# Deferring the gating of the first two channel tiles of a ConvFFN by one tile, and pinning four low halves to other places

## The chip, the cores and the metric

The kernel runs on one core of a Trainium2 chip. The metric is the device time of one execution in microseconds; before, three runs gave a median of 1300.59 us (1300.02 to 1301.46). The engines are called here as in the profile: PE (TensorE's matrix multiplications), PEld (its weight loads), DVE (VectorE), ACT (ScalarE), POOL (GpSimd) and SP (SyncE, which issues most DMAs).

## The reference, cut to what matters

One decoder layer in float32 on 16 meta tokens and 1024 tokens, model width 1024. The part that the change touches is the end of the mixing block and the ConvFFN:

```
mix = concat([y_diff, y_hgrn]) @ w_out                # out projection, 1024 x 1024
h   = h + rmsnorm(mix, ln_mix_post)
a   = rmsnorm(h, ln_ffn_pre)
u   = a @ w_ffn_up                                    # 1024 -> 2 * 2816
u   = causal depthwise conv over tokens, width 3, + conv_b
gate, up = split(u)
y   = (gelu_tanh(gate) * up) @ w_ffn_down             # 2816 -> 1024
h   = h + rmsnorm(y, ln_ffn_post)
```

`y_diff` is a differential attention with four heads, `y_hgrn` a gated linear recurrence (HGRN2) with four heads; both are computed ahead of this part.

## The kernel before

**Products in three passes.** Each float32 operand of a multiplication is split into a high half in the PE's reduced format (a cast on ACT, `uh`, `woh`, `t` high) and a low half, raw minus high (a subtraction on DVE or POOL, `ul`, `wol`, `t` low; the function `split`). A product is three matmuls, high times high, high times low and low times high (lines 1398, 1399 and 1400 in the up projection, 1028, 1030 and 1032 in the out projection). The low halves are wanted a matmul or two after the high ones.

**The out projection.** `load_wo(n)` loads column half n of `w_out` in eight tiles `wor{n}_{k}` and splits them into `woh{n}_{k}` and `wol{n}_{k}`. PE's products `py` and `pz` of half 0 run in gaps of the recurrence (whose gate products `hq`, `kr` are made by DVE and read by the small matmuls `pl`, `pd`); half 1 follows near 565 us of the profile. The recurrent heads' decay factors `tt`, `t2` are on POOL.

**The up projection.** The 2816 channels are 22 tiles of 128, each with a gate and an up side, and the tokens are two halves, p = 0 (2 x 258 columns) and p = 1 (2 x 256). Tile 0 is done plainly: `plain_unit` makes `pq` in four products for each token half, and ACT copies them to `ug0_p` and `uu0_p`. Tiles 1 to 21 use a fast 2 x 2 block scheme with seven products instead of eight (`unit`): `prep(7*ft + j)` makes the weight operand of product j of tile ft (`uh`, `ul`; the sums `ws1` to `ws4` of raw quarter tiles `ra{ft}_{11,12,21,22}` are POOL's), and `t_sums` and `t_split` make the eight token operands `t{p}_{j}` once, from the transposed activations `at2_p`. The products use three PSUM banks for each token half, in this order of j: `pa`, `pb`, `pc`, `pb`, `pa`, `pb`, `pc`. From the fourth on they accumulate on what lies in the bank, so between two products in one bank an engine has to have read it:

- j = 0 `pa`: ACT copies it to `xu`
- j = 1 `pb`: DVE adds it to `xu` (the trace's `xu<-pb,xu`), before j = 3 may write `pb`
- j = 3 `pb`: DVE makes `u3` (the trace's `u<-pb,xu`) and, with `pc` of j = 2, half of `uu`; j = 5 waits for `u3`
- j = 4 `pa`, j = 5 `pb`, j = 6 `pc`: the other halves of `ug` and `uu`

**Gating.** `gated(ft, p, ug, uu)` takes the finished outputs of a tile and a token half through the convolution: `conv` for each side, an ACT activation (bias and one tap) and two DVE steps (SCALAR_TENSOR_TENSOR, one tap each) in `c0` and `c1`, then the gelu on ACT, the product `c0*c1` on POOL and the store to `gsc` by SP. That is four DVE steps for each call, eight for each tile. `c1` has two buffers, `c0` three.

**What sets the order.** PE's order is written out by the order of the code (`unit` yields after each product, and the loop over `ft` and `j` interleaves two token halves). The order on DVE, ACT, POOL and SP is a scheduler's, over the same code; `tc.issue_after(ins)` holds what is issued inside behind the instruction given. All element-wise work goes through one helper and bears line 58. In before, the loop calls `gated` of a tile at its end, after j = 6, for all tiles; for tile 0 `plain_unit` calls it, token half 0 ahead of the loop and half 1 at j = 1 of tile 1. The weights of tile 2 (`prep(14)` on) are made in places of their own during tile 1:

```
if (ft, j) == (1, 1):
    with tc.issue_after(marks[1, 1].ins):
        next(p1)
    with tc.issue_after(marks["mult"].ins):
        prep(14)
elif ft == 1 and 2 < j < 6:
    with tc.issue_after(marks["last"].ins):
        prep(12 + j)
```

**The down projection** reads the gates back from `gsc` (`g_in`, tiles `gi` with tag `gk` in the pool `dn`), splits them and multiplies with `w_ffn_down` (`pd`).

## Time and profile before

| | |
|---|---|
| time, median of 3 runs (lowest to highest) | 1300.59 us (1300.02 to 1301.46) |
| profiled execution: its own time, its span | 1298.48 us, 1296.7 us |
| mean granted PE clock | 0.993 |
| PE busy | 1261.1 us, 97% |
| DVE busy | 885.1 us, 68% |
| ACT busy | 693.2 us, 53% |
| POOL busy | 485.4 us, 37% |

In the profile a row of a timeline gives the start, the duration, the engine, the line, the operation and its tiles (output<-inputs, buffer numbers left out), a count where neighbours are taken together, and in square brackets the idle time ahead of it and what ended it. The view of waits groups such idle time by the waiting line and the releasing engine: microseconds in total, times, longest. The view by windows gives for each stretch its length, then the busy time of PE, PEld, DVE, ACT and POOL with the number of instructions, the granted PE clock, the DMA share and GB/s. A difference between starts is the better measure of what one operation costs in a train, since durations of neighbours overlap a little. Of the profiled execution the up projection takes roughly from 627 to 1050 us.

### The profile page before, as it was taken

How to read it: one execution, taken by the hardware profiler on the slowest of the kernel's cores; microseconds unless marked ns; L12 is line 12 of the kernel's file. 1: busy time of each engine (PE TensorE's matmuls, PEld its weight loads, DVE VectorE, ACT ScalarE, POOL GpSimd, SP SyncE). 2: the span in 40 equal slices, each digit the busy share in tenths (PEclk: the TensorE clock that was granted, in tenths of full speed). 3: DMA queues.
4: the chain of work that ended last, by engine and by line, in shares of the span. 5: the costliest groups of instructions: out<-in, count | busy, mean ns of one | idle time of the engine just before them, and what ended most of it. 6: DMA issues, size and time to landing. Idle time of an engine off the chain costs nothing.

```text
span 1296.7 us, 26036 instructions
## 1 busy us (share of the span) xinstructions
PE 1261.1 (97%) x10154; PEld 1174.8 (91%) x10154; DVE 885.1 (68%) x1488; ACT 693.2 (53%) x1639; POOL 485.4 (37%) x387
## 2 busy tenths in 40 slices
PE   8999999999999999999997999999999999999996
PEld 7999999999999998768897999999999998878885
DVE  7574646464746564547887778778778786797686
ACT  8465466546654754356754445444445454454553
POOL 5231423242323310352076665765766730010121
PEclk9999999999999999999998999999999999999998
DMA  7335555273634532787322222222222147955363
GB/s 256 95 66 123 88 144 93 74 144 99 122 91 79 123 86 98 247 271 249 112 66 74 82 74 91 82 74 87 85 75 90 66 139 240 343 173 170 90 211 122
DMA packets 116417, 165.04 MB, mean 127 GB/s; under 512 B 10099, under 2 KB 57523, under 8 KB 116294
## 3 DMA queue, kind: packets, MB, share of 16 engines
q1 hardware_dynamic: 93062, 151.84, 36.2%
q0 software_dynamic: 23232, 11.54, 7.5%
q8 instruction: 80, 1.31, 0.4%
q14 instruction: 43, 0.35, 0.1%
HBM read 134.24 MB, written 52.17 MB: 144 GB/s over the span
## 4 chain that ended last, share of the span: by engine, by line
PE 44%; DVE 6%; ACT 2%; issue 1%; DMA 1%; POOL 0%; DVEq 0%; SPq 0%; ACTq 0%; POOLq 0%
PE pd L1567 5%; PE pd L1568 5%; PE pd L1566 5%; PE pb L1398 4%; PE pb L1399 4%; PE pb L1400 4%; PE pa L1399 3%; PE pc L1399 3%; PE pa L1398 3%; PE pc L1398 3%; PE pa L1400 3%; PE pc L1400 3%; DVE c L58 1%; DVE t L58 1%; DVE xh L58 1%
## 5 line engine op out<-in xcount | busy, mean ns | idle before, releaser
L1398 PE MATMUL pb<-t,uh 128*128 128x258 f32 x504 | 142.0, 282 | 8.2 <-DVE xu L58 8.2
L1399 PE MATMUL pb<-t,uh 128*128 128x258 f32 x504 | 142.2, 282 | 0.0
L1400 PE MATMUL pb<-t,ul 128*128 128x258 f32 x504 | 141.4, 281 | 0.0
L1567 PE MATMUL pd<-wl,gh 128*128 128x512 f32 x308 | 120.5, 391 | 1.1 <-DVE wl L58 1.1
L1566 PE MATMUL pd<-wh,gh 128*128 128x512 f32 x308 | 120.0, 390 | 0.0
L1568 PE MATMUL pd<-wh,gl 128*128 128x512 f32 x308 | 120.0, 390 | 0.0
L58 POOL TENSOR_TENSOR c<-c,c 128x514 f32<-128x514 f32 (+1 forms) x44 | 64.2, 1459 | 122.2 <-ACT c L58 118.1
L58 DVE SCALAR_TENSOR_TENSOR c<-uu,cwt,c 128x514 f32<-128x514 f32 (+1 forms) x88 | 95.6, 1087 | 20.5 <-ACT c L58 19.8
L1398 PEld LDWEIGHTS pb<-t,uh 128*128 128x128 f32 x504 | 96.1, 191 | 8.6 <-DVE xu L58 8.6
L1399 PEld LDWEIGHTS pb<-t,uh 128*128 128x128 f32 x504 | 96.1, 191 | 0.0
L1400 PEld LDWEIGHTS pb<-t,ul 128*128 128x128 f32 x504 | 96.1, 191 | 0.0
L1399 PE MATMUL pa<-t,uh 128*128 128x258 f32 (+1 forms) x336 | 94.2, 280 | 0.0
L1399 PE MATMUL pc<-t,uh 128*128 128x258 f32 (+1 forms) x336 | 94.1, 280 | 0.0
L1398 PE MATMUL pa<-t,uh 128*128 128x258 f32 (+1 forms) x336 | 93.9, 279 | 0.0
L1398 PE MATMUL pc<-t,uh 128*128 128x258 f32 (+1 forms) x336 | 93.7, 279 | 0.0
L1400 PE MATMUL pa<-t,ul 128*128 128x258 f32 (+1 forms) x336 | 93.7, 279 | 0.0
L1400 PE MATMUL pc<-t,ul 128*128 128x258 f32 (+1 forms) x336 | 93.6, 278 | 0.0
L58 DVE SCALAR_TENSOR_TENSOR c<-ug,cwt,c 128x514 f32<-128x514 f32 (+1 forms) x88 | 86.2, 980 | 1.2 <-ACT c L58 0.6
L58 ACT CAST uh<-ra 128x512 fp32r<-128x512 f32 x67 | 41.1, 616 | 64.6 <-PE pb L1399 40.2
L58 DVE TENSOR_TENSOR ul<-ra,uh 128x512 fp32r<-128x512 f32 x42 | 40.6, 967 | 47.0 <-ACT uh L58 44.5
L58 POOL TENSOR_TENSOR ul<-ws,uh 128x512 fp32r<-128x512 f32 x42 | 60.2, 1435 | 30.8 <-ACT uh L58 30.8
L1567 PEld LDWEIGHTS pd<-wl,gh 128*128 128x128 f32 x308 | 57.8, 188 | 14.7 <-DVE wl L58 2.8
(389 smaller groups left out, 4171.1 us busy)
## 6 DMA issues: line engine op xcount, KB each, us to landing
ra<-in_wup_dram SPq DMA_DIRECT2D x88, 256.0 KB, 2.8
mp<-msc SPq DMA_DIRECT2D x23, 512.0 KB, 5.8
tsc<-in_wdown_dram SPq DMA_DIRECT2D x44, 256.0 KB, 4.7
wi<-tsc SPq DMA_DIRECT2D x44, 256.0 KB, 3.2
gi<-gsc SPq DMA_DIRECT2D x33, 256.0 KB, 4.6
wi<-in_wdown_dram SPq DMA_DIRECT2D x33, 256.0 KB, 4.8
gsc<-c SPq DMA_DIRECT2D x22, 257.0 KB, 2.1
tsc<-in_wdown_dram POOLq DMA_DIRECT2D x22, 256.0 KB, 6.7
```

The costliest lines, as they stand in the source:

```text
L58: ins = call(*args, **kw)
L1398: T.matmul(pt, hi[:, s], th[:, k], start=(first and k == 0), stop=False, skip_group_check=True)
L1399: T.matmul(pt, hi[:, s], tl[:, k], start=False, stop=False, skip_group_check=True)
L1400: T.matmul(pt, lo[:, s], th[:, k], start=False, stop=(k == 3), skip_group_check=True)
L1566: T.matmul(py, gh[:, s], wh, start=(k == 0 and pr not in (3, 7)), stop=False, skip_group_check=True)
L1567: T.matmul(py, gh[:, s], wl, start=False, stop=False, skip_group_check=True)
L1568: T.matmul(py, gl[:, s], wh, start=False, stop=(k == NH - 1), skip_group_check=True)
```

## The change

The change leaves every computation as it is, and PE's order too. It moves work on the other four engines:

- **Gating of tiles 0 and 1.** The calls of `gated` for tile 0 and tile 1 are put on a list (`later`) and taken from it in the next tile: tile 0's in tile 1 and tile 1's in tile 2, token half 0 after j = 1 and half 1 after j = 3, each held behind the DVE operation that evacuates the product (`marks["last"]`). Tile 2 on gate themselves at their end, as before. So in tile 2 both tile 1's gating and its own are issued.
- **Where tile 1's outputs lie.** `ug1_p` and `uu1_p` are taken from the `gk` tiles of the pool `dn` (four buffers, made 516 wide for it), which otherwise hold gates loaded for the down projection.
- **Weights of tile 2** are prepared by the ordinary calls in the loop; the special places are gone.
- **Low halves pinned.** `wol0_4` to `wol0_7` move from DVE to POOL; the low half of product 4 of tile 1 (`ul11`) moves from POOL to DVE; `prep(7)` to `prep(10)` are held behind the low halves `wol1_4` and `wol1_5`; among the token operands, the lows of quarters `t1_7` and `t1_6` are held ahead of the sums of token half 0 (`t0_2`, `t0_3`, `t0_5`).

On DVE, around product 3 of tile 1 (`xu_1_p` read the bank of product 1, `u3_1_0` that of product 3; `c0_0_0` and `c1_0_0` are the plain tile's convolution steps). Before:

```order
L58 TENSOR_TENSOR ul14_8083<-ra2_11_8072,uh14_8082 128x512
L58 SCALAR_TENSOR_TENSOR c0_0_0_7972<-ug0_0_7645,cwt_84,c0_0_0_7972 128x514
L58 SCALAR_TENSOR_TENSOR c1_0_0_7977<-uu0_0_7646,cwt_84,c1_0_0_7977 128x514
L58 SCALAR_TENSOR_TENSOR c0_0_0_7972<-ug0_0_7645,cwt_84,c0_0_0_7972 128x514
L58 SCALAR_TENSOR_TENSOR c1_0_0_7977<-uu0_0_7646,cwt_84,c1_0_0_7977 128x514
L58 TENSOR_TENSOR xu_1_0_7999<-pb1_0_8033,xu_1_0_7999 128x258
L58 TENSOR_TENSOR xu_1_1_8017<-pb1_1_8047,xu_1_1_8017 128x256
L58 SCALAR_TENSOR_TENSOR c0_0_1_8061<-ug0_1_7825,cwt_84,c0_0_1_8061 128x510
```

and in the changed kernel, from the same low half on:

```order
L58 TENSOR_TENSOR ul14_7997<-ra2_11_7986,uh14_7996 128x512
L58 TENSOR_TENSOR xu_1_0_8003<-pb1_0_8037,xu_1_0_8003 128x258
L58 TENSOR_TENSOR xu_1_1_8021<-pb1_1_8051,xu_1_1_8021 128x256
L58 SCALAR_TENSOR_TENSOR c0_0_0_8065<-ug0_0_7645,cwt_84,c0_0_0_8065 128x514
L58 SCALAR_TENSOR_TENSOR c1_0_0_8070<-uu0_0_7646,cwt_84,c1_0_0_8070 128x514
L58 SCALAR_TENSOR_TENSOR c0_0_0_8065<-ug0_0_7645,cwt_84,c0_0_0_8065 128x514
L58 SCALAR_TENSOR_TENSOR c1_0_0_8070<-uu0_0_7646,cwt_84,c1_0_0_8070 128x514
L58 TENSOR_TENSOR ul15_8079<-ws2_8076,uh15_8078 128x512
L58 TENSOR_TENSOR ul17_8115<-ws3_8112,uh17_8114 128x512
L58 TENSOR_TENSOR u3_1_0_8004<-pb1_0_8037,xu_1_0_8003 128x258
```

The two evacuations have moved ahead of the four steps, and two low halves of tile 2 now stand between the steps and `u3_1_0`; the plain tile's other four steps come behind `u3` and `uu`.

On DVE, around product 3 of tile 2 (`xu_2_0`), with the steps of tile 1 (`c0_1_p`, `c1_1_p`). Before:

```order
L58 TENSOR_TENSOR ug1_1_8015<-pc1_1_8099,xu_1_1_8017 128x256
L58 SCALAR_TENSOR_TENSOR c0_1_0_8235<-ug1_0_7997,cwt_84,c0_1_0_8235 128x514
L58 SCALAR_TENSOR_TENSOR c1_1_1_8264<-uu1_1_8016,cwt_84,c1_1_1_8264 128x510
L58 SCALAR_TENSOR_TENSOR c0_1_1_8259<-ug1_1_8015,cwt_84,c0_1_1_8259 128x510
L58 TENSOR_TENSOR ul21_8281<-ra3_11_8270,uh21_8280 128x512
L58 SCALAR_TENSOR_TENSOR c0_1_1_8259<-ug1_1_8015,cwt_84,c0_1_1_8259 128x510
L58 TENSOR_TENSOR xu_2_0_8286<-pb2_0_8320,xu_2_0_8286 128x258
L58 TENSOR_TENSOR ul22_8351<-ws2_8348,uh22_8350 128x512
```

and in the changed kernel:

```order
L58 TENSOR_TENSOR ul22_8341<-ws2_8338,uh22_8340 128x512
L58 TENSOR_TENSOR xu_2_1_8283<-pb2_1_8313,xu_2_1_8283 128x256
L58 SCALAR_TENSOR_TENSOR c0_1_0_8327<-ug1_0_8000,cwt_84,c0_1_0_8327 128x514
L58 SCALAR_TENSOR_TENSOR c1_1_0_8332<-uu1_0_8001,cwt_84,c1_1_0_8332 128x514
L58 SCALAR_TENSOR_TENSOR c0_1_0_8327<-ug1_0_8000,cwt_84,c0_1_0_8327 128x514
L58 SCALAR_TENSOR_TENSOR c1_1_0_8332<-uu1_0_8001,cwt_84,c1_1_0_8332 128x514
L58 TENSOR_TENSOR ul24_8377<-ws3_8374,uh24_8376 128x512
L58 TENSOR_TENSOR u3_2_0_8266<-pb2_0_8299,xu_2_0_8265 128x258
```

All eight steps of tile 1 stood ahead of `xu_2_0`, the last of them are shown; now `xu_2_0` comes ahead of `ul22`, four steps stand between `xu_2_1` and `u3_2_0`, and the other four behind the evacuations of product 3.

On POOL, at the turn from the out projection to the weights of tile 1 (`wol1_4` is a low half of `w_out`, the rest are sums and a low half of tile 1's weights). Before:

```order
L58 TENSOR_TENSOR wol1_6_7044<-wor1_6_7041,woh1_6_7043 128x512
L58 TENSOR_TENSOR ws1_7819<-ra1_21_7815,ra1_22_7813 128x512
L58 TENSOR_TENSOR ws2_7853<-ws1_7819,ra1_11_7811 128x512
L58 TENSOR_TENSOR ul9_7886<-ws1_7819,uh9_7885 128x512
L58 TENSOR_TENSOR wol1_4_7032<-wor1_4_7029,woh1_4_7031 128x512
L58 TENSOR_TENSOR ws3_7915<-ra1_11_7811,ra1_21_7815 128x512
```

and in the changed kernel:

```order
L58 TENSOR_TENSOR wol1_6_7044<-wor1_6_7041,woh1_6_7043 128x512
L58 TENSOR_TENSOR wol1_4_7032<-wor1_4_7029,woh1_4_7031 128x512
L58 TENSOR_TENSOR ws1_7819<-ra1_21_7815,ra1_22_7813 128x512
L58 TENSOR_TENSOR ws2_7853<-ws1_7819,ra1_11_7811 128x512
L58 TENSOR_TENSOR ws3_7915<-ra1_11_7811,ra1_21_7815 128x512
L58 TENSOR_TENSOR ul9_7886<-ws1_7819,uh9_7885 128x512
```

`wol1_4` has moved ahead of two sums and a low half; on ACT its cast stands ahead of that of `uh9` likewise.

The diff:

```diff
--- before.py
+++ after.py
@@ -156,6 +156,7 @@
             low = (eng or G).tensor_tensor(lo, raw, hi.bitcast(F32), op=ALU.subtract)
         if eng in (None, G):
             lows.append(low)
+        return low
 
     def load_split(src, name, where=None, bufs=4):
         raw = wp.tile([P, 512], F32, tag="wr", name=f"wr_{name}", bufs=WR)
@@ -996,6 +997,8 @@
     ssy = yp.tile([P, NBLK, 4], F32, tag="ssy", name="ssy")
     gpo0 = yp.tile([P, 512], F32, tag="gpo0", name="gpo0")
 
+    wo_low = {}
+
     def load_wo(n):
         res = []
         for k in range(KD):
@@ -1010,10 +1013,10 @@
                 hi = wop.tile([P, 512], F32R, tag="woh", name=f"woh{n}_{k}")
                 lo = wop.tile([P, 512], F32R, tag="wol", name=f"wol{n}_{k}")
             if n == 0:
-                split(hi, lo, raw, V if k else G)
+                split(hi, lo, raw, V if 0 < k < 4 else G)
             else:
                 with tc.issue_after(ends["a"].ins), tc.issue_after(ends["v"].ins):
-                    split(hi, lo, raw, V if k % 2 else G, halved[0])
+                    wo_low[k] = split(hi, lo, raw, V if k % 2 else G, halved[0])
             res.append((hi, lo))
         return res
 
@@ -1167,7 +1170,7 @@
         where = swp if q % 2 else wp
         hi = where.tile([P, 512], F32R, tag="wh", name=f"uh{q}", bufs=4)
         lo = where.tile([P, 512], F32R, tag="wl", name=f"ul{q}", bufs=4)
-        split(hi, lo, src, G if j % 2 == 0 and j else V, marks.get((ft - 1, 0)) if j == 1 else None)
+        split(hi, lo, src, G if j % 2 == 0 and j and (ft > 1 or j != 4) else V, marks.get((ft - 1, 0)) if j == 1 else None)
         made[q] = (hi, lo)
 
     plain = {}
@@ -1262,8 +1265,8 @@
 
     def t_split(p, j, src, where, *tag):
         hi, lo = t_tiles(p, j, where, tag)
-        A.copy(hi, src)
-        V.tensor_tensor(lo, src, hi.bitcast(F32), op=ALU.subtract)
+        marks["cast"] = A.copy(hi, src)
+        marks["low"] = V.tensor_tensor(lo, src, hi.bitcast(F32), op=ALU.subtract)
         tt[p][j] = (hi, lo)
 
     def quarter(p, j):
@@ -1273,15 +1276,21 @@
 
     def t_sums(p, where, last):
         b11, b12, b21, b22 = (quarter(p, j) for j in (0, 7, 4, 6))
-        V.tensor_tensor(b11, b12, b11, op=ALU.subtract)
+        cast, low = marks["quarters"]
+        with tc.issue_after(low.ins) if p else nullcontext():
+            V.tensor_tensor(b11, b12, b11, op=ALU.subtract)
         V.tensor_tensor(b12, b22, b12, op=ALU.subtract)
         V.tensor_tensor(b22, b22, b11, op=ALU.subtract)
         for j, b in ((1, b22), (2, b11), (3, b12)):
             if p == 0:
                 gap(where, f"gap4{j}", 128 if j == 1 else 192)
-            t_split(p, j, b, where, f"t{p}_{j}")
+            with nullcontext() if p or j == 1 else tc.issue_after(cast.ins):
+                with nullcontext() if p or j == 1 else tc.issue_after(low.ins):
+                    t_split(p, j, b, where, f"t{p}_{j}")
         V.tensor_tensor(b21, b21, b22, op=ALU.subtract)
-        t_split(p, 5, b21, *last)
+        with nullcontext() if p else tc.issue_after(cast.ins):
+            with nullcontext() if p else tc.issue_after(low.ins):
+                t_split(p, 5, b21, *last)
 
     def run(*args):
         for _ in out_part(*args):
@@ -1345,6 +1354,8 @@
     gap(tp, "gap1", 128)
 
     def outputs(ft, p):
+        if ft == 1:
+            return [dn.tile([P, 2 * WN[0]], F32, tag="gk", name=f"{t}{ft}_{p}") for t in ("ug", "uu")]
         return [xup.tile([P, 2 * WN[0]], F32, tag=t, name=f"{t}{ft}_{p}") for t in ("ug", "uu")]
 
     def conv(ft, p, side, u):
@@ -1379,13 +1390,14 @@
                         T.matmul(pt, lo[:, s], th[:, k], start=False, stop=(kh == 1 and k == 3))
                 A.copy(us[side][:, col * n:(col + 1) * n], pt)
                 yield
-        gated(0, p, *us)
-        yield
+        later.append((0, p, *us))
 
     def unit(ft, p, bank):
         n = WN[p]
         nm = f"{ft}_{p}"
         ug, uu = outputs(ft, p)
+        if (ft, p) == (1, 0):
+            gap(dn, "gap7", 384)
         pair = mxp.tile([P, 768], F32, tag="ms", name=f"xu_{nm}", bufs=2)
         x1, u2 = pair[:, :n], pair[:, WN[0]:WN[0] + n]
         u3 = xup.tile([P, WN[0]], F32, tag="u3", name=f"u3_{nm}")[:, :n]
@@ -1422,8 +1434,13 @@
         yield
         mm(6, pc, False)
         marks["last"] = V.tensor_tensor(ug[:, n:2 * n], pc, u2, op=ALU.add)
-        gated(ft, p, ug, uu)
+        if ft == 1:
+            later.append((ft, p, ug, uu))
+        else:
+            gated(ft, p, ug, uu)
         yield
+
+    later = []
 
     p0 = plain_unit(0, ps_b)
     next(p0)
@@ -1435,20 +1452,25 @@
     trans(8)
     t_split(1, 7, quarter(1, 7), tp, "t1_5")
     t_split(1, 6, quarter(1, 6), mxp, "X0", MIX["X0"])
+    marks["quarters"] = marks["cast"], marks["low"]
     t_sums(0, tp, (mxp, "X2", MIX["X2"], 16))
     close(a_cms.pop())
     t2_cm, t2p = pool("tsplit2", 1)
     gap(t2p, "gap2", 64)
     p1 = plain_unit(1, ps_b)
     for j in range(4):
-        prep(7 + j)
+        with tc.issue_after(wo_low[5].ins), tc.issue_after(wo_low[4].ins):
+            prep(7 + j)
         next(p1)
     t_sums(1, t2p, (tp, "t1_5"))
     close(a_cms.pop(), b_cm)
     v_cm, cv = pool("conv", 2, "right")
     gap(cv, "gap3", 416)
     dn_cm, dn = pool("down", 4, "right")
-    next(p0)
+    for _ in p0:
+        pass
+    for _ in p1:
+        pass
     for j in range(4, 7):
         prep(7 + j)
 
@@ -1461,7 +1483,7 @@
         return gsc[P * k: P * (k + 1), 512 * half: 512 * (half + 1)]
 
     def g_in(k, half, nm):
-        t = dn.tile([P, 512], F32, tag="gk", name=f"gi{nm}_{k}")
+        t = dn.tile([P, 2 * WN[0]], F32, tag="gk", name=f"gi{nm}_{k}")[:, :512]
         SY.dma_start(t, g_src(k, half))
         return t
 
@@ -1507,19 +1529,14 @@
     for ft in range(1, NF):
         units = [unit(ft, p, ps_b) for p in range(2)]
         for j in range(7):
-            if j != 1 and (ft > 1 or j > 3):
+            if j != 1:
                 prep(7 * (ft + 1) + j)
             for u in units:
                 next(u)
-            if (ft, j) == (1, 1):
-                with tc.issue_after(marks[1, 1].ins):
-                    next(p1)
-                with tc.issue_after(marks["mult"].ins):
-                    prep(14)
-            elif ft == 1 and 2 < j < 6:
+            if ft < 3 and j in (1, 3):
                 with tc.issue_after(marks["last"].ins):
-                    prep(12 + j)
-            elif j == 1:
+                    gated(*later.pop(0))
+            if j == 1:
                 prep(7 * (ft + 1) + j)
             if ft == NF - 2 and j == 5:
                 with tc.issue_after(marks["store"].ins):
```

## The prediction

> **What bounds the kernel now.** I read the page's busy shares first, then the waits of TensorE, then TensorE's timeline where the longest wait lies, and then the timelines of the engines it waits for.
>
> ```profile
> PE 1261.1 (97%) x10154; PEld 1174.8 (91%) x10154; DVE 885.1 (68%) x1488; ACT 693.2 (53%) x1639; POOL 485.4 (37%) x387
> PE pb L1398 <- DVE xu L58: 8.2, 2, 6.8
> PE py L1030 <- POOL wol L58: 2.2, 1, 2.2
> PE pq L1378 <- DVE t L58: 1.8, 1, 1.8
> PE pl L473 <- DVE am L58: 1.1, 1, 1.1
> ```
>
> TensorE is busy for 97% of the span and its order of work is the same before and after, so only its idle time and its clock can change. The four waits hold 13.3 us; the 8.2 is 6.83 and 1.39. All lie between 515 and 690 us, where the out projection turns into the up projection, and there the change works.
>
> ```profile
> 647.63 0.38 PE L1378 MATMUL pq<-t,uh 128*128 128x256 f32 x1 [1.79 <-DVE t L58]
> 655.86 0.28 PE L1398 MATMUL pb<-t,uh 128*128 128x258 f32 x1
> 658.65 0.28 PE L1398 MATMUL pc<-t,uh 128*128 128x258 f32 x1
> 663.00 0.39 PE L1398 MATMUL pb<-t,uh 128*128 128x258 f32 x1 [1.39 <-DVE xu L58]
> 679.86 0.28 PE L1398 MATMUL pc<-t,uh 128*128 128x258 f32 x1
> 689.64 0.58 PE L1398 MATMUL pb<-t,uh 128*128 128x258 f32 x1 [6.83 <-DVE xu L58]
> 694.95 0.42 PE L1398 MATMUL pa<-t,uh 128*128 128x258 f32 x1
> 698.07 0.28 PE L1398 MATMUL pb<-t,uh 128*128 128x258 f32 x1
> 712.04 0.28 PE L1398 MATMUL pb<-t,uh 128*128 128x258 f32 x1
> ```
>
> These are first matmuls of products. Undisturbed, one product (both token halves) takes 658.65 − 655.86 = 2.79 us. The row at 689.64 is product 3 of channel tile 2; after the product at 679.86 it could have begun at 682.65, so it came 6.99 late. It then took 5.31 to the next, and that one 3.12: 2.52 and 0.33 too long.
>
> ```profile
> 560.00:600.00 40.00, 37.84 (x172) 28.99 (x171) 25.37 (x28) 23.29 (x67) 22.05 (x16) 1.00 0.80 267
> 660.00:680.00 20.00, 18.61 (x161) 18.41 (x160) 15.89 (x21) 9.15 (x16) 15.54 (x12) 1.00 0.34 107
> 680.00:690.00 10.00, 3.17 (x26) 2.98 (x25) 10.00 (x11) 3.80 (x9) 6.68 (x5) 0.77 0.16 56
> 690.00:700.00 10.00, 10.00 (x65) 10.00 (x65) 4.13 (x9) 2.83 (x6) 8.04 (x6) 0.72 0.31 94
> ```
>
> In this view by windows the number ahead of the DMA share is the granted clock. It fell to 0.72 behind the 6.83 wait and stayed 1.00 around the 2.16 wait. So the long wait cost 6.99 + 2.52 + 0.33 = 9.84 us, 2.85 of it clock. [...]
>
> **Why VectorE is late.**
>
> ```profile
> 638.37 6.93 DVE L58 TENSOR_TENSOR t<-at,t 128x1024 fp32r<-128x1024 f32 x6
> 646.35 2.36 DVE L58 TENSOR_TENSOR t<-at,t 128x1024 fp32r<-128x1024 f32 x2
> 657.17 0.69 DVE L58 TENSOR_TENSOR ul<-ra,uh 128x512 fp32r<-128x512 f32 x1
> 659.49 1.78 DVE L58 SCALAR_TENSOR_TENSOR c<-uu,cwt,c 128x514 f32<-128x514 f32 x1
> 661.20 0.74 DVE L58 SCALAR_TENSOR_TENSOR c<-ug,cwt,c 128x514 f32<-128x514 f32 x1
> 662.53 0.74 DVE L58 TENSOR_TENSOR xu<-pb,xu 128x258 f32<-128x258 f32 x2
> 679.10 3.14 DVE L58 SCALAR_TENSOR_TENSOR c<-uu,cwt,c 128x514 f32<-128x514 f32 x2
> 688.52 0.74 DVE L58 SCALAR_TENSOR_TENSOR c<-ug,cwt,c 128x510 f32<-128x510 f32 x1
> 689.18 0.41 DVE L58 TENSOR_TENSOR xu<-pb,xu 128x258 f32<-128x258 f32 x1
> 699.71 0.43 DVE L58 TENSOR_TENSOR uu<-pb,xu 128x258 f32<-128x258 f32 x1 [0.21 <-PE pb L1400]
> 710.57 0.41 DVE L58 TENSOR_TENSOR xu<-pb,xu 128x258 f32<-128x258 f32 x1
> ```
>
> Product 3 accumulates on the bank of product 1, so it waits until `xu` has read that bank; the matmul starts 0.46 after `xu` does (689.18 to 689.64). `xu` of tile 2 stands behind the eight convolution steps of tile 1, whose last is the row at 688.52. A step is 0.66 alone (two from 661.20 to 662.53) and about 1.57 (3.14 for two) to 1.78 where GpSimd works beside it. `xu` itself, with an operand in PSUM, is 0.41 in all these rows.
>
> ```profile
> 563.54 1.62 POOL L58 TENSOR_TENSOR ws<-ra,ra 128x512 f32<-128x512 f32 x1
> 566.49 1.28 POOL L58 TENSOR_TENSOR ul<-ws,uh 128x512 fp32r<-128x512 f32 x1
> 567.73 1.71 POOL L58 TENSOR_TENSOR wol<-wor,woh 128x512 fp32r<-128x512 f32 x1
> 652.05 6.97 POOL L58 TENSOR_TENSOR ul<-ra,uh 128x512 fp32r<-128x512 f32 x1 [47.06 <-ACT uh L58]
> 676.57 1.73 POOL L58 TENSOR_TENSOR ws<-ra,ra 128x512 f32<-128x512 f32 x1 [0.26 <-DMA ra<-in_wup_dram]
> 683.34 1.71 POOL L58 TENSOR_TENSOR ws<-ra,ws 128x512 f32<-128x512 f32 x1
> ```
>
> GpSimd's operation is 1.28 alone. From 676.57 to 683.34 it began four more, one each 1.69 us, while VectorE's steps went at 1.57: they alternate, a pair in about 1.65. Behind the train of 1024-wide VectorE operations it got no turn at all (the 6.97 ends when that train does). [...]
>
> **The change part by part**, on the time axis of before.
>
> *Costing nothing.* Tile 1's outputs lie in the tiles that later hold loaded gates: no instruction more, and those loads come only ahead of the down projection. The stores to `gsc` come later by one channel tile; they are read in the down projection. The row counts are nearly those of before, so work is moved, not added.
>
> *The wait of 2.16 at 567.* The low half `wol1_4` ran at 567.73 on GpSimd behind the sums and `ul9` (563.54 to 567.73). Now it stands ahead of them, right behind `wol1_6`, and its cast ahead of `uh9`: it is done near 566, before TensorE needs it. Gain 2.16. The sums `ws1` to `ws4` come about 1.7 later; they feed weights of tile 1, first used after 650, so nobody waits. Behind them come the gains on `y0`, now with three sums of tile 2 among them.
>
> ```profile
> 590.66 1.65 POOL L58 TENSOR_TENSOR y<-y,gpo 128x512 f32<-128x512 f32 x1 [6.31 <-ACT jz L58]
> 592.96 0.53 SPq L1056 DMA_DIRECT2D mp<-msc  x1
> 675.53 0.82 ACT L58 ACTIVATE c<-uu,cbt,cwt 128x514 f32<-128x514 f32 x1 [1.12 <-DVE uu L58]
> ```
>
> Those need 3 × 1.28 = 3.84 and stand in the 6.31 that GpSimd waited there. On SP the load `ra2_12` now stands ahead of one of `mp1_6` (592.96) and waits for the last of these sums, which is done near 590.66 − 6.31 + 3.84 = 588.2: no cost.
>
> *Around 515.*
>
> ```profile
> 513.11 0.69 DVE L58 TENSOR_TENSOR wol<-wor,woh 128x512 fp32r<-128x512 f32 x1 [3.79 <-ACT woh L58]
> 513.72 1.23 DVE L58 TENSOR_TENSOR hq<-hq,f 128x1040 f32<-128x1040 f32 x1
> ```
>
> The gate product `hq` stood behind `wol0_6`, which stood 3.79 behind a cast. With that low half on GpSimd, `hq` is free and the 1.06 of `pl` goes. But TensorE now needs the low half from GpSimd, 1.28 to 1.7 instead of 0.69: 0.6 to 1.0 later, in the same microseconds. Between −0.1 and +1.1 I take a gain of 0.5.
>
> *The wait of 1.79 at 645.8.* The lows `t1_7`, `t1_6` (646.35, two) now come ahead of three of the six at 638.37. The wait goes. The train as a whole gains `ul11` (0.6) and about 0.4 of waiting for the cast of `t1_7`; so it ends at 657.86 + 1.0 = 658.9 (657.17's end is 657.86). `t1_1`, late in it, comes near 656.5; TensorE, now 1.79 earlier, wants it at 655.9. New wait 0.6.
>
> *Convolutions behind the evacuations: tile 1.* `xu` runs at 658.9, TensorE wants it at 660.25. The 1.39 goes. Product 5 needs `u3` of product 3, and that one is now behind four steps of the plain tile and the lows `ul15`, `ul17`. GpSimd has `ul13`, `ws4`, `ul16`, `ws1` ready beside them: four pairs of 1.65 minus the head start, 659.7 to 665.7, then 0.6 for `ul15` and 1.5 for `ul17` beside `ws2`: `u3` at 667.8, the matmul at 668.25. It is due at 660.25 + 2 × 2.79 = 665.85. New wait 2.4; with the steps alone at 0.66 it would be none.
>
> *Tile 2.* The steps for the plain tile's second half run from 669.3 to 673.7, `ul19` after them; `uu` and `ug` of tile 1 follow by 675.7. Now ScalarE's queue is in front: its copy of tile 2's product 0 stands behind the biases of tile 1's convolutions, of which `c1_1_1` waits until GpSimd's product `c_0_1` has freed its buffer. That product starts behind the last step, at 673.7, and takes 1.7; behind it are three biases of some 0.75 (675.53's 0.82 with its overlap), and two casts of half a microsecond and more: the copy is at 679.0 and `xu` at 679.7; TensorE wants it at 668.25 + 5 × 2.79 = 682.2. So the wait of 6.83 and its clock go, with some 2 us to spare. Then `ul22`, four steps of tile 1 (681.0 to 685.9) and `ul24`, which waits for a cast behind the gelu: `u3` of tile 2 at 687.9, matmul at 688.35, due 687.8: new wait 0.5.
>
> *Tile 3.* After `u3` come four more steps (689.3 to 692.9), `ul26` and at 694.2 `uu` of product 5. From that `uu` to the next `xu` VectorE needs 710.57 − 699.71 = 10.86 in before, for the same list of work, since tile 2 gates itself as before. So `xu` of tile 3 is at 705.1, the matmul at 705.55; due is 688.35 + 5 × 2.79 = 702.3. New wait 3.25. From here on the order is that of before, and TensorE's waits were none: the shift stays to the end.
>
> *Sum.* Product 3 of tile 3 begins at 705.55 instead of 712.04: 6.5 us. With 2.16 and 0.5 from earlier the gain is 9.2. The profiled execution took 1298.48 and would take 1289.3; the three runs' median is 2.1 above that execution, so I forecast 1300.59 − 9.2 = **1291.4**. No clock loss is in it: 3.25 lies between 2.16 (none) and 6.83 (2.85), nearer the first. [...]
>
> **The rivals.**
>
> *A, VectorE keeps up.* If most steps run at 0.66, because GpSimd is held up by buffers and casts rather than always ready, only the 0.6 at `t1_1` stays. Product 3 of tile 3 would then be at 705.55 − 2.4 − 0.5 − 3.25 = 699.4, the gain 12.6 + 2.7 = 15.3, the time 1285.3. For it: before 669 two of four steps did run at 0.66. Against: less idle VectorE time is left for GpSimd to use.
>
> *B, the long wait moves to tile 3.* The backlog of eight steps is only deferred into tile 2. If it is 2 us greater than walked, the last wait is over 5, the clock falls and adds up to 2.85: gain 9.2 − 4.9 = 4.3, time 1296.3. For it: the walk's pairs are taken at 1.65, and 0.2 more for ten of them does it. [...]
>
> *C, slower.* GpSimd collides with every step and low half between 659 and 705. Some 32 of VectorE's operations there have both operands in SBUF; the walk gives its sixteen steps 1.2 each. With the clock's 2.85, the time is 0.2% (2.6 us, about what a measurement can tell from no change) above before when tile 3's `xu` is 9.2 + 2.6 − 2.85 = 9 us later than walked, 0.28 more for each operation; at 1.57 for all it is 12 later, giving 1300.59 − 9.2 + 12 + 2.85 = 1306. Against: in before GpSimd had 12 + 5 + 6 = 23 operations from 660 to 700, and each can delay only one of the 32.
>
> *D, the move does nothing*, if `xu` of tile 2 is held as long by ScalarE's copy (behind `c_0_1` on GpSimd) as by the steps now: 1300. The walk leaves 2.5 us.
>
> **How the numbers follow.** Chances: forecast (1288 to 1293.5) 0.53, A 0.18, B (to 1297.9) 0.19, D 0.04, C 0.06. Faster by over 0.2% are forecast, A and B, 0.90; same 0.04; slower 0.06. The range reaches from A's end into B's, 1285.5 to 1297; outside it are D, C and the fringes of A and B, not quite 2 in 10.
>
> **What would show it.** Right: no wait of `py` for `wol` near 567; waits of `pb` for `xu` of tile 2 gone; granted clock 1.00 from 680 to 700; short waits of `pb` for `u` and, near 700, for `xu`. A has none of these; B shows one long wait near 700 with a clock under 0.8. Wrong: a wait over 4 us at any product of tiles 1 to 3, a wait for ScalarE's copy, or GpSimd's low halves late (`pa`, `pc` waiting for `ul`).

## The result and the profile after

The changed kernel takes 1294.39 us (median of 10 runs, 1292.39 to 1298.38) against 1298.93 for the kernel before in the same rounds: a ratio of 0.9965 (0.9953 to 0.9977), a gain of 4.5 us (3.0 to 6.1). A second series gave 0.9958 (0.9946 to 0.9971). The forecast was 9.2. The profiled execution took 1292.96 us, 5.52 less than that of before.

The busy shares on the page, and then the waits of TensorE in the view of waits (total, times, longest), of the changed kernel:

```profile
PE 1259.6 (98%) x10154; PEld 1173.5 (91%) x10154; DVE 887.3 (69%) x1485; ACT 694.3 (54%) x1639; POOL 490.8 (38%) x390
```

```profile
PE pb L1410 <- DVE xu L58: 4.0, 1, 4.0
...
PE pa L1250 <- DVE a L58: 1.6, 1, 1.6
...
PE py L1035 <- issue: 1.2, 1, 1.2
```

The waits of before (6.83 and 1.39 for `xu`, 2.16 for `wol`, 1.79 for `t`, 1.06 for `am`) are gone. In their place stand one of 3.97 for `xu`, now of channel tile 3, one of 1.6 for the normalised activations `a`, and one of 1.2 that the profile ascribes to nothing ("issue").

TensorE's timeline of the changed kernel, at the same points of its order of work (lines are shifted by a few: 1398 is now 1410, 1030 is 1033, 1247 is 1250):

```profile
515.08 0.70 PE L474 MATMUL pl<-hq,kr 128*32 128x16 f32 x62
527.25 0.39 PE L1035 MATMUL py<-woh,mp 128*128 128x512 f32 x1 [1.23 <-issue]
573.60 0.40 PE L1031 MATMUL pz<-woh,m 128*2 128x512 f32 x1
606.13 1.09 PE L1250 MATMUL pa<-ident,a 128*128 128x128 f32 x8 [1.62 <-DVE a L58]
640.00 0.37 PE L1388 MATMUL pq<-t,uh 128*128 128x256 f32 x1
656.30 0.39 PE L1411 MATMUL pb<-t,uh 128*128 128x256 f32 x1 [0.82 <-DVE t L58]
667.01 0.39 PE L1410 MATMUL pb<-t,uh 128*128 128x258 f32 x1 [0.79 <-DVE u L58]
681.09 0.28 PE L1410 MATMUL pb<-t,uh 128*128 128x258 f32 x1
704.78 0.39 PE L1410 MATMUL pb<-t,uh 128*128 128x258 f32 x1 [3.97 <-DVE xu L58]
709.26 0.28 PE L1410 MATMUL pa<-t,uh 128*128 128x258 f32 x1
```

Against before, `pl` is 1.03 ahead at 515.08 (516.11), but the product at 527.25 is 0.33 behind (526.92). `pz` is 1.76 ahead at 573.60 (575.36), but at 606.13 the lead is gone (606.12) and `pq` at 640.00 starts where it did (640.03). So everything won ahead of 640 was lost again by 640. From there on the change does what it was expected to: product 3 of tile 2 (681.09) no longer waits, and product 3 of tile 3 begins at 704.78 instead of 712.04, 7.26 ahead. It then takes 4.48 to the next product instead of 2.79, so 5.57 remain, and 5.52 is what the whole execution gained.

Why 4.48? The view by windows of TensorE alone (length, busy time with the number of matmuls, granted clock, DMA share, GB/s), cut at 3.413 us:

```profile
698.91:702.32 3.41, 1.90 (x17) 1.00 0.00 0
702.32:705.74 3.42, 0.96 (x8) 1.00 0.46 154
705.74:709.15 3.41, 3.41 (x19) 0.50 0.20 77
709.15:712.56 3.41, 3.41 (x31) 1.00 0.00 0
```

The clock was exactly half for exactly one such stretch, right behind one in which TensorE was idle for 2.45 of it. Half of 3.41 is 1.71, and the product took 4.48 − 2.79 = 1.69 too long. The stretches are not an arbitrary choice, as the last part of the experiments shows.

### The profile page after: what moved, and what is told of

Read it like the earlier page. It is cut to its first block, busy times and chain, and to the rows that moved or that the text cites. A ratio compares the mean times of both kernels' runs of the same rounds, so it can differ in the third digit from the quotient of the medians.

```text
span 1291.1 us, 26037 instructions
## 1 busy us (share of the span) xinstructions
PE 1259.6 (98%) x10154; PEld 1173.5 (91%) x10154; DVE 887.3 (69%) x1485; ACT 694.3 (54%) x1639; POOL 490.8 (38%) x390
## 4 chain that ended last, share of the span: by engine, by line
PE 46%; DVE 6%; issue 2%; ACT 1%; DMA 0%; POOL 0%; DVEq 0%; SPq 0%; POOLq 0%; ACTq 0%
PE pd L1584 5%; PE pd L1585 5%; PE pd L1583 5%; PE pb L1410 4%; PE pb L1411 4%; PE pb L1412 4%; PE pc L1411 3%; PE pc L1410 3%; PE pc L1412 3%; PE pa L1411 3%; PE pa L1410 3%; PE pa L1412 3%; DVE c L58 2%; DVE t L58 1%; PE pa L1250 0%
## 5 line engine op out<-in xcount | busy, mean ns | idle before, releaser
L58 POOL TENSOR_TENSOR ul<-ws,uh 128x512 fp32r<-128x512 f32 x42 | 65.3, 1555 | 78.3 <-ACT uh L58 73.9
```

What stands on the lines that cost most here:

```text
L58: ins = call(*args, **kw)
```

## The experiments

Ratios are to the kernel before, measured in the same rounds (medians 1299.56, 1299.49 and 1300.45).

**The two halves of the change, each alone on the kernel before.** e_out_only keeps the pinned low halves and drops the deferred gating; e_gate_only the reverse. The gating half has the weights of tile 2 made by the ordinary calls, and with them it brings GpSimd's sums of tile 2 forward to some 585 us; e_out_only leaves these sums where before has them.

Of e_out_only:

```diff
-                split(hi, lo, raw, V if k else G)
+                split(hi, lo, raw, V if 0 < k < 4 else G)
...
-        prep(7 + j)
+        with tc.issue_after(wo_low[5].ins), tc.issue_after(wo_low[4].ins):
+            prep(7 + j)
```

and of e_gate_only:

```diff
+            if ft < 3 and j in (1, 3):
                 with tc.issue_after(marks["last"].ins):
-                    prep(12 + j)
+                    gated(*later.pop(0))
```

> Before, with only the pinning of the low halves (wol0_4 to wol0_7 on GpSimd, wol1_4 ahead of the sums, ul11 on VectorE, t1_7 and t1_6 ahead of the sums of token half 0); the gating of tiles 0 and 1 as in before. No sums of tile 2 move. Theory 1: the wait of 2.16 at 567 and the 1.79 at 646 go and, without the moved sums, the gain of some 1.6 us at 600 is kept; the long wait for xu of tile 2 stays near 7 us with a clock under 0.8, since VectorE's backlog of tile 1 is the same, and swallows what was gained ahead of it only as far as VectorE's work itself starts no earlier: time 0 to 3 us under before. Rival (the pinning is worth its whole 2.7 us plus 1.8 to the end): 4 us or more under before.

> Before, with only the deferral of the gating of tiles 0 and 1 (outputs of tile 1 in the gate tiles, weights of tile 2 by the ordinary calls); the low halves where before had them, so the waits at 515, 567 and 646 are all there. Theory 1 (the gain of the change is the gating alone, 5.5 us in the profile): 4 to 6.5 us under before, with the wait of 6.8 us for xu of tile 2 gone and one of 3 to 4.5 us at tile 3, and a wait of over 2.5 us near 606 or 567, since the sums of tile 2 collide here too. Rival (both parts are needed, as VectorE starts tile 1 later without the pinning): under 3 us.

e_out_only: 0.9977 (0.9968 to 0.9986), 1296.85 us. e_gate_only: 0.9977 (0.9968 to 0.9987), 1297.43 us. Each half is worth about 3.0 us by its ratio, and the two together would make 0.9954, within the interval of the whole (0.9953 to 0.9977), so the times don't show that one undoes the other. e_gate_only missed its theory's 4 to 6.5 us. In it the wait for `xu` of tile 2 is gone and one of 4.2 stands at tile 3, like the changed kernel's, and TensorE waits 2.5 us in all for `a` between 590 and 634. In e_out_only the wait for `xu` of tile 2 is 7.2 as before, the 2.16 at 567 is gone, and there is a wait "issue" of 3.2 at 528.

**The gains at 515 and 567, and the sums ahead of the `y0` gains.** In the changed kernel's timelines of GpSimd and VectorE, at 590:

```profile
586.42 2.14 POOL L58 TENSOR_TENSOR ws<-ws,ra 128x512 f32<-128x512 f32 x1
588.53 1.29 POOL L58 TENSOR_TENSOR ws<-ra,ra 128x512 f32<-128x512 f32 x1
589.78 1.74 POOL L58 TENSOR_TENSOR y<-y,gpo 128x512 f32<-128x512 f32 x1
588.54 1.82 DVE L58 SCALAR_TENSOR_TENSOR xh<-y,ssy,xh 128x512 f32<-128x512 f32 x1
590.29 1.78 DVE L58 SCALAR_TENSOR_TENSOR xh<-tmp,ssy,xh 128x512 f32<-128x512 f32 x1
```

The sums of tile 2 and the gain run beside the steps `xh` of the normalisation, which take 1.8 instead of the 0.75 of before (at 589.74 and 590.41). `a` is made at 594.65 in both kernels. e_sums_late holds the sums behind the last gain:

```diff
+        with tc.issue_after(marks["gain"].ins) if ft == 2 else nullcontext():
-        G.tensor_tensor(sums[nm], a, b, op=op)
+            G.tensor_tensor(sums[nm], a, b, op=op)
...
-            y0_gain(i)
+            marks["gain"] = y0_gain(i)
```

> The changed kernel, but GpSimd's three weight sums of tile 2 (ws1 to ws3) stand behind the last of the y0 gains instead of between the fourth and the fifth; nothing else moves but one weight load on SP behind them. Theory 1 (the sums collide with VectorE's residual steps near 588 to 592 and so eat the gain made at 567): those two steps fall back from 1.8 us to about 0.7 each, the wait of the transposes for the normalised block near 606 (1.6 us in the changed kernel) falls under 0.5, and the time is 1.0 to 1.7 us less than the changed kernel's, so near 7 us under before in the profile. Rival (the chain of normalisations paces TensorE there whatever GpSimd does): the wait stays at 1.3 to 1.7 and the time does not move.

It took 1295.11 us, 0.9958 (0.9946 to 0.9971): no gain over the changed kernel. The wait at 606 is gone (TensorE also comes there some 1.5 us later, after longer waits at 527 and 556) and these `xh` steps are at 0.75 again. But the sums now run from 604.70 on, beside the next pair of `xh` steps, which take 0.74 each in before (606.59 and 607.25):

```profile
606.35 1.16 DVE L58 SCALAR_TENSOR_TENSOR xh<-y,ssy,xh 128x512 f32<-128x512 f32 x1
607.43 1.77 DVE L58 SCALAR_TENSOR_TENSOR xh<-tmp,ssy,xh 128x512 f32<-128x512 f32 x1
```

The next `a` comes 1.2 later than in before (610.98 against 609.77), and the transposes wait for `a` of later token blocks:

```profile
620.25 1.09 PE L1251 MATMUL pa<-ident,a 128*128 128x128 f32 x8 [0.64 <-DVE a L58]
630.77 1.09 PE L1251 MATMUL pa<-ident,a 128*128 128x128 f32 x8 [0.22 <-DVE a L58]
```

So this edit moved the contention and didn't remove it; it can't tell what the lead is worth without it. e_out_only can, as its expectation foresaw, since its kernel doesn't bring these sums forward. In its second execution (the run for the clock, below) TensorE is 1.04 ahead of before at the `pz` of 573.60, still 1.05 ahead at the `pq` of 640.00, and the view of waits from 570 to 645 is empty:

```profile
574.32 0.40 PE L1031 MATMUL pz<-woh,m 128*2 128x512 f32 x1
638.98 0.37 PE L1386 MATMUL pq<-t,uh 128*128 128x256 f32 x1
```

In its first execution it is 1.39 behind before at both places. In e_gate_only, which brings the sums forward and wins no lead, 0.94 behind becomes 3.84 behind. So the lead of 1.76 was taken by the sums of tile 2, wherever they meet `xh`. Before itself, run again, lost 0.7 there in one execution, so the chain has little slack even without them. No run has the whole change with these sums where before has them, so what that would be worth in time was not measured.

**Spreading the backlog.** The wait at tile 3 arises because tile 1's gating and tile 2's own both stand in tile 2. e_spread defers half of tile 2's by one more tile:

```diff
-        if ft == 1:
+        if ft == 1 or (ft, p) == (2, 1):
             later.append((ft, p, ug, uu))
...
-            if ft < 3 and j in (1, 3):
+            if ft < 3 and j in (1, 3) or (ft, j) == (3, 3):
```

> The changed kernel, but tile 2 gates only its first token half at its end; its second half is deferred into tile 3 (behind product 3), so tile 2 carries twelve convolution steps instead of sixteen and tile 3 twelve instead of eight. Theory 1 (the 3.97 wait of product 3 of tile 3 is the doubled load of tile 2, which VectorE's idle share of about 4 us a tile can take in two parts): xu of tile 3 comes 3.5 to 5 us earlier, ahead of TensorE; at tile 4 a wait of 0 to 1.5 us is left, the granted clock stays 1.00, and the time is 4 to 5.5 us under the changed kernel's. Rival (VectorE is late there for the sum of its work, and any deferral only hands the wait on): the wait appears at tile 4 with 3 us or more, and the time changes by less than 1.5 us.

It took 1290.58 us, 0.9929 (0.9915 to 0.9942), the fastest version of this study; run again it gave 0.9938 (0.9922 to 0.9955; its expectation is quoted further below). TensorE's timeline of e_spread around tile 3:

```profile
700.75 0.39 PE L1410 MATMUL pb<-t,uh 128*128 128x258 f32 x1 [0.17 <-DVE xu L58]
703.34 0.39 PE L1410 MATMUL pb<-t,uh 128*128 128x256 f32 x1 [0.89 <-DVE xu L58]
713.60 0.38 PE L1410 MATMUL pc<-t,uh 128*128 128x256 f32 x1 [1.58 <-DVE uu L58]
```

The 3.97 and its 1.71 of clock became 0.17 + 0.89 + 1.58 = 2.64 with the clock at 1.00: 3.04 less. The two kernels were not timed in the same rounds; by their ratios they gain 4.5 and 9.2 us over before, and 5.5 and 8.1 when run again. This shows the late part of the account: VectorE's backlog in tile 2 sets the end of the gain.

**Both repairs, and one more step.** e_spread_sums joins e_spread and e_sums_late; e_all_mended also puts tile 3's second token half in `gk` tiles, so that its `uu` need not wait for a buffer (`if ft == 1 or (ft, p) == (3, 1)` in `outputs`).

> Both edits on the changed kernel: tile 2's second half deferred into tile 3, and GpSimd's three sums of tile 2 behind the last y0 gain. In the first series the sums alone gave no clear time, since the wait of 4 us at tile 3 and the clock behind it differ from run to run. Theory 1 (the sums' collision near 590 is worth what the profile shows, the 1.6 us wait near 606): without that noise 0.8 to 1.6 us under the kernel with the spread alone, which stood at 0.9929 of before, so 0.992. Rival (those 1.6 us are found again in later waits of the normalisation or of the first tile): within 0.4 us of the spread alone.

> As the kernel with spread and late sums, but the outputs of tile 3's second token half lie in the gate tiles. With the spread alone TensorE waited 1.6 us at product 6 of tile 3 for uu, whose buffer was still held by tile 2's outputs. Theory (a buffer, not VectorE's load): that wait goes, xu of tile 4 stays ahead of TensorE or up to 1 us late, and the time is 0.5 to 1.6 us less than without it, near 0.991 of before. Rival (VectorE is the limit there, and the wait moves to xu of tile 4): the same time, with a wait of 1 to 2 us at product 3 of tile 4.

e_spread_sums: 1291.46 us, 0.9938 (0.9925 to 0.9951), no gain over e_spread. e_all_mended: 1292.93 us, 0.9953 (0.9940 to 0.9965), worse by its median, though the intervals overlap: the 1.58 for `uu` goes, and 2.10 for `xu` of tile 4 comes, with half a clock behind it. The backlog moves on once more, as the rival had it. e_spread_sums settles nothing about the sums either, since they are held behind the last gain as in e_sums_late.

**The changed kernel and the kernel before, once more**, for the spread of the short waits and of the clock.

> The changed kernel as it is, beside the others on one chip. Its ten runs went from 1292.4 to 1298.4 where those with the spread stayed within 1.0 us. Theory (the wait at tile 3 is near 4 us, after which the clock falls for a time that differs from run to run): the runs spread over 2 us and more again, the profile shows the wait of 3.9 to 4.0 and behind it 1.5 to 3 us of slow matmuls. Rival (that spread was the chip of those runs): within 1.5 us.

> Before as it is, a second profile. In the changed kernel and in all four edits TensorE waited 0.8 to 3.2 us near 527 for something that the profile does not name, and not in before. Theory (it is the landing of a load of the out projection's operand, issued near 519 and 6 to 9.5 us under way, which TensorE meets later if the gate wait ahead of it is there): a wait of 0 to 1 us at that place, as the landing falls. Rival (something the change brought): none at all. The wait of 6.8 us at tile 2 and a clock of 0.7 to 0.8 behind it are there again.

1294.03 us (0.9958, 0.9946 to 0.9971) and, in a single run, 1299.16. The wait "issue" was 1.52 in the first and 0.50 in the second: the change did not bring it. The waits for `xu` were 3.97 and 7.13.

**The wait near 527.** The first theory was a wait for a load of activations, behind four loads of weights in SyncE's queue. e_load_first, on e_spread, puts those four behind it:

```diff
-            last_load.append(SY.dma_start(raw, wout[...]))
+            with tc.issue_after(loads[4].ins) if n else nullcontext():
+                last_load.append(SY.dma_start(raw, wout[...]))
```

> The kernel of e_spread, with SyncE's loads of the next four tiles of the out projection's weight (wor1_0 to wor1_3) put behind the two loads of the fourth activation block and those of the fifth, instead of ahead of them; nothing else moves. Theory, that the gain of about 1 us at 515 is handed back near 527 because TensorE's products py catch up with the second load of that block, which stands in SyncE's queue behind those four (each waits for a buffer that a low half frees), and behind a store: the load is issued some 2 us or more before 517.5, the wait of 0.8 (up to 3.2 in other runs) of py near 527 goes, the block's product starts within 1 us of when the one before it ends, and the time falls by 0.8 to 1.5 us against e_spread run beside it, with a narrower spread. Rival, that the wait has another cause (the store's own landing, which stays ahead of the load): the wait stays within 0.5 us of what e_spread shows beside it and the time stays within 0.5 us.

> The kernel of e_spread once more, as the measure for e_load_first on the same chip and for its own spread: 1289.5 to 1291.5 us, a wait of 0.5 to 1.5 us of py near 527, no wait over 2 us after 650 us and a granted clock of 1.00 from 560 to 1050 us by either theory. If its earlier gain over the changed kernel (3.8 us) was chance, it is 1293 to 1295.

No gain: 1292.51 us (0.9939, 0.9920 to 0.9957) beside 1292.62 of e_spread_again. The latter missed its own ranges too: its median lies between the two that its expectation gave, its wait near 527 was 2.47, and half a clock came at 609. The edit alone could not test the theory, because SyncE issues the loads behind the store no earlier (517.70 here, 516.62 in e_spread_again), and the wait is there:

```profile
517.70 2.73 SPq L1060 DMA_DIRECT2D mp<-msc  x3
528.60 0.39 PE L1036 MATMUL py<-woh,mp 128*128 128x512 f32 x1 [1.64 <-issue]
```

But the traces speak against any load. The matmul that starts late is the same in every execution with the wait, and the profile names nothing that it waits for ("issue"); its weight load had run at 525.96 in the changed kernel. The load issued near 519 lands anywhere from 2.4 us before that matmul to 0.7 us after it. What fits better is the queue q8 in the page's part on DMA queues (packets, MB, share), and in the same view of the changed kernel from 524.8 to 526.0 us:

```profile
q8 instruction: 80, 1.31, 0.4%
```

```profile
q8 instruction: 1, 0.02, 5.1%
```

80 packets of 16 KB stand beside 20,308 matmuls and weight loads, one for every 254; that they carry TensorE's own instructions is an estimate from this ratio and the queue's name, and no trace shows it. In all fourteen executions one such packet starts between 523.9 and 526.0, near trains of short matmuls (`pl`, 128x16, 62 of them in 0.70 us at 525.29 of the changed kernel). In the twelve with the wait TensorE goes on 1.3 to 1.6 us after its end (1.5 in the changed kernel), however long the wait was (0.50 to 3.17); in the two without (before, and e_mended_again below) it ended 1.2 us or more before TensorE was due. That the packet causes the wait is argued from this coincidence; no run moved the packet.

**The clock.** These are the half-clock intervals between 480 and 780 us in the first twelve executions. Each lasts 3.41, 6.83 or 10.24 us, and two in one execution lie a whole number of 3.413 us apart (160.43 = 47 of them in e_out_only). That execution, in the view by windows of TensorE:

```profile
524.10:527.51 3.41, 1.10 (x68) 1.00 0.75 243
527.51:530.93 3.42, 2.56 (x7) 0.50 0.16 58
530.93:534.34 3.41, 3.41 (x71) 0.50 0.00 0
...
684.53:687.94 3.41, 0.00 (x0) 1.00 0.22 79
687.94:691.36 3.42, 1.00 (x5) 0.50 0.36 112
691.36:694.77 3.41, 3.41 (x17) 0.50 0.32 120
```

So there is a fixed grid, at another place in each execution. On it, every full-clock stretch with 2.10 us or more of idle time (ten of them) is followed by one at half clock, and none with 1.93 or less, but for one place below. A stretch at half clock with 0.85 of idle time or more is followed by another, one with 0.12 or less by full clock. From 14 to 1270 us of before, the changed kernel, e_spread, e_spread_sums and e_all_mended there is no half clock outside 480 to 780, and between 480 and 780 none of the fourteen executions departs from these limits but at the one place below. Three pairs of rows show how little the length of a wait says. Before, the 2.16 that cost nothing:

```profile
565.85:569.26 3.41, 1.48 (x7) 1.00 0.98 272
569.26:572.68 3.42, 3.19 (x14) 1.00 0.87 255
```

e_spread_again, a wait of 2.47 that cost nothing, since the grid cut it in two (1.79 and 0.67):

```profile
523.66:527.07 3.41, 1.62 (x71) 1.00 0.74 243
527.07:530.49 3.42, 2.74 (x23) 1.00 0.30 105
```

e_all_mended, a wait of 2.10 inside one stretch, which cost 1.71:

```profile
723.17:726.59 3.42, 1.32 (x11) 1.00 0.35 124
726.59:730.00 3.41, 3.41 (x18) 0.50 0.31 110
```

Two kernels were run again to test this rule.

> The kernel of e_out_only once more, for its clock alone. Theory, read from the traces so far: the clock is decided on a fixed grid of 3.413 us that lies differently in each execution; a stretch of the grid in which TensorE is idle for 2.0 us or more is followed by one stretch at half clock (each costing 1.7 us of work), one with 1.9 or less by none. So the half-clock intervals near 528 and 690 are whole multiples of 3.41 us, their starts differ by a whole multiple of it (within 0.05), and the 7.2 us wait of pb for xu costs two or three stretches by where the grid lies. [...]

> The kernel of e_all_mended once more, for its clock alone. Theory of the grid: the waits of about 2.1 (pb for xu of tile 4) and 0.5 to 3 (py near 527) are followed by half clock only where 2.0 us or more of one of them lie in one stretch of the grid of 3.413 us; half-clock intervals are 3.41 or 6.83 us long and start on one grid. For the wait of 2.1 that is so in somewhat under half of all positions of the grid. Rival, a limit on the length of one wait: 2.1 us is followed by half clock again, as in the run before (if the limit is under 2.1), whatever the grid.

They took 1296.08 and 1292.48 us (one run each). The windows of e_out_only_again, then of e_mended_again:

```profile
681.90:685.31 3.41, 0.00 (x0) 1.00 0.26 79
685.31:688.73 3.42, 0.81 (x4) 0.50 0.37 124
688.73:692.14 3.41, 3.41 (x18) 0.50 0.29 108
```

```profile
720.37:723.79 3.42, 1.29 (x11) 1.00 0.42 149
723.79:727.20 3.41, 3.41 (x18) 0.50 0.25 89
```

Both follow the rule: two stretches for the wait of 7.3, one for 2.13 of idle time within one stretch. In e_out_only_again the wait near 528 was only 1.6 and was followed by none, so the common grid had one interval to show there, not two. The second run alone would also fit a limit just under 2.1 on a wait; the 2.47 above does not.

The exception is at 606. There e_load_first had only 1.22 idle, and half clock behind it (so had e_spread_again, with 1.28 in the stretch):

```profile
605.07:608.48 3.41, 2.19 (x19) 1.00 0.61 169
608.48:611.90 3.42, 3.42 (x9) 0.50 0.98 376
```

Most of what shows as busy in that stretch are transposes (from 606.67 to 608.34). It would fit if these counted for less than other matmuls: if 0.45 to 0.75 of the time of matmuls with the identity is taken as idle, one limit near 2.0 separates all stretches at full clock, also the one of the changed kernel where 1.62 of idle time and 0.6 of transposes were followed by full clock. That is an estimate fitted to these traces afterwards; no run tests it.

## Why the prediction was right in direction and its gain twice too large

**Right: the tiles 1 to 3.** VectorE's timeline of the changed kernel, for the rows that the walk placed:

```profile
658.50 0.76 DVE L58 TENSOR_TENSOR xu<-pb,xu 128x258 f32<-128x258 f32 x2
666.55 0.74 DVE L58 TENSOR_TENSOR u<-pb,xu 128x258 f32<-128x258 f32 x2
679.20 0.41 DVE L58 TENSOR_TENSOR xu<-pb,xu 128x258 f32<-128x258 f32 x1
693.48 0.41 DVE L58 TENSOR_TENSOR uu<-pb,xu 128x258 f32<-128x258 f32 x1
704.31 0.41 DVE L58 TENSOR_TENSOR xu<-pb,xu 128x258 f32<-128x258 f32 x1
```

`xu` of tiles 1, 2 and 3 was placed at 658.9, 679.7 and 705.1, `uu` of tile 2 at 694.2: each 0.4 to 0.8 too late. The 10.86 from that `uu` to the next `xu`, carried over from before, came out as 10.83. The new waits were set at 0.6, 2.4, 0.5 and 3.25 and are 0.8, 0.8, 0 and 3.97. The 2.4 was the worst: `u3` came at 666.55, not 667.8. That error cost the sum nothing, because VectorE's backlog, not TensorE's place, sets the last start; a shorter wait earlier only makes the last one longer. This part was sized at 6.5 and is 7.26. Rival A's "VectorE keeps up" is out: it keeps up in tile 2 and not in tile 3.

**Wrong: "Gain 2.16" at 567 and "I take a gain of 0.5" at 515.** Both waits did go (1.76 and 1.03 of lead), and both leads were gone within 33 us. For the first, the failing step is that the sums of tile 2 were put at no cost: "stand in the 6.31 that GpSimd waited there" asks whether GpSimd has time, and not what its work does to VectorE beside it, though the prediction itself had measured a pair of the two at 1.65. The `xh` steps took 1.8 instead of 0.75, `a` came no earlier than in before, and where the sums don't come forward (e_out_only) the lead lasts. For the second, the failing step is that the lead was carried to the end without asking what TensorE meets next: near 527 it waited in twelve of fourteen executions, and went on 1.3 to 1.6 us behind a packet of the queue q8, whatever its lead had been. The cause of that wait stays open. Together 2.66 of the 9.2.

**Wrong: "No clock loss is in it".** I set the limit by the lengths of two waits, 2.16 and 6.83, and took 3.25 as "nearer the first". The length is not what decides. By the rule that the runs showed, with the limit taken as 2.0 (it lies between 1.93 and 2.10), a wait of L between 2 and 4 us has, by an estimate from this limit and the grid's 3.41, 2 us in one stretch for (L − 2 + 1.41)/3.41 of all positions of the grid: 0.78 for 3.25, 0.99 for 3.97. The term should have been 1.3 to 1.7, and 1.71 was lost. The sum, by the profile: 9.2 − 2.66 − 1.71 + 0.76 = 5.6, against 5.52. Rival B's time (1296.3) lay nearer than the forecast, but not for its reason: VectorE was 0.8 earlier than walked, not 2 later, and the clock fell all the same. That the stated range held the result, in the part given to B, is therefore partly luck.

## What to carry to other kernels

Follow a lead to the next place where TensorE meets another chain before adding it to a sum: two of three terms here (1.76 and 1.03 of lead) were won and lost again. Idle time of one engine is not a free place for work that slows its neighbour: the sums that filled GpSimd's idle time here took back what another part of the same change had won (`xh` steps of 1.8 us instead of 0.75). Work taken off a busy engine's critical moment came back here as a backlog in the next tiles; spread over two tiles it cost 2.64 instead of 5.68, and with the wait for a buffer taken out it came back in tile 4 (2.10). A wait of between 2 and 4 us, as far as these runs show, should be priced with the chance of half a clock for a whole stretch of 3.41 us behind it (1.71 behind the 3.97 and behind a 2.10); cutting it in two short ones can save that loss even where the idle time stays (none behind the 2.47 that lay as 1.79 and 0.67 in two stretches).

## What the runs showed of the hardware that was not expected

In these executions the granted clock changed on a grid of 3.413 us that was fixed within each of them: 2.10 us of idle time or more in one stretch was followed by half the clock for the next, 1.93 or less was not (but for the stretch of transposes at 606, with 1.22 and 1.28), at a cost of 1.71 us where the halved stretch was filled with work. Since the grid lies at another place in each execution, this can be a part of the spread between runs of one kernel (1292.39 to 1298.38 for the changed kernel); no run shows how large a part. TensorE stood still for 0.5 to 3.2 us near 527 in twelve of fourteen executions, and went on each time 1.3 to 1.6 us behind a packet of the queue q8; that the packet is the cause is not shown. Steps of VectorE on 128x512 that took 0.75 in before took 1.16 to 1.82 with GpSimd's sums and a gain beside them, in two places, and delayed TensorE through the normalisation.
